# DeltaNet masks and output sums as PSUM accumulation, inverse copies on ScalarE

## The chip, the core and the metric

## The reference, cut to what matters

The model is a two-layer backbone over 512 latent and 256 context tokens, width 1024: a gated DeltaNet layer, then an attention layer, each followed by a mixer that picks experts by product keys. The change touches the DeltaNet layer's recurrence, which runs for 16 value heads of width 128, forwards and backwards in time, over chunks of tokens:

```python
gc = cumsum(gc)
decay = exp(where(incl, gc[:, None] - gc[None, :], -inf))     # incl: lower triangle
kk = k @ k.T
a = eye + where(strict, kk * decay * b[:, None], 0)
u, w = triangular_solve(a, [v * b, k * (b * exp(gc))])
v_new = u - w @ S
qk = where(incl, (q @ k.T) * decay, 0)
o = (q * exp(gc)) @ S + qk @ v_new
S = S * exp(g_last) + (k * exp(g_last - gc)).T @ v_new
```

The outputs of the forward and the backward direction are added. The state S left by the context is where the latents start.

## The kernel before

Everything is fp32; the large products outside the recurrence are split into two fp32r parts. The program is traced in one order and a scheduler places each engine's instructions by a model of their times, so an instruction can stand earlier or later on its engine than the text has it. Each engine then works through its own list in order. Tiles come from pools with a fixed number of buffers, and a write to a reused buffer waits for its last reader.

Chunks here are 128 tokens: 2 for the context, 4 for the latents. `dn_rec` (line 423) is called once for the context ("c") and once for the latents ("l"). It takes the 8 query/key heads in groups, 4 heads a group for the context and 2 for the latents, so that a group always holds 16 matrices per direction to invert. There are two groups for the context and four for the latents. The tiles of odd and even groups come from different pools, so that a group can be prepared while the group before it is still in its steps. The work on a group has four parts:

- Preparation, chunk by chunk (lines 450 to 472). `kk` in PSUM receives k·k and k·q (L453). VectorE multiplies both by the two triangle masks `tri` into `km` (L456), one mask per direction. `rp` in PSUM receives, for two value heads and two directions, the row of cumulated gates by a transpose of a broadcast column (L462). ScalarE forms `ar` = exp(-relu(gc - rp)) (L466, L467). VectorE multiplies into `U`, the matrix to invert (L470, four instructions), and `Ps` (named `Pm` in the rows), the masked and decayed k·q (L472).
- `dn_inv` (line 575): the inverse of I + U for 16 matrices and two directions at once. ScalarE gathers the 32x32 diagonal blocks (L585), VectorE transposes and eliminates them in 31 dependent steps (L596, L598) and transposes back (L602, L603). TensorE then builds the off-diagonal blocks with ScalarE copies between (`Tc`, `T6`), and VectorE copies the inverted diagonal blocks back into `U` (L639).
- `dn_step` (line 517), for each chunk, head and direction: `ks` = k·S and q·S (L529), `R` (L532), `yr` by the inverse (L540, L541), `vd` and `vn` (L545, L547), the state update `su` and `S` (L550, L555). Then `q`, the scaled q·S (L561, into `o` itself for the direction that comes first to a chunk, else into `qs`), `ops` = Ps·vn (L564), and VectorE's sums: q + ops (L571), and o + q for the direction that comes second (L573). In the context the first step of each direction has no state, and its `ops` are copied to `o` by ScalarE (L567).
- The end of a group: `o` is normalised (L503, L507), transposed (L513), multiplied by the gate `zt` loaded from memory (L510, L514), and stored (L515). `ZT` (8, 4) gives the buffers of `zt` for the context and the latents.

Beside the recurrence runs a background queue of gathers for the experts of the context. `tick` (line 55) is called at fixed places of the loops and issues gather steps by a rate. A step is an indirect DMA of 128 rows of 4 KB on GpSimd's queue (L965), into one of `GB` = 4 row buffers, and a VectorE instruction that reduces the row block against the tokens (L967).

The PSUM of `dn_rec` is one buffer each of `kk`, `rp` and `mg`, two of `ks`, and one each of `yr`, `su` (which shares with the transposes `tp`) and `ops`.

## Time and profile before

| | us |
|---|---|
| median of three runs | 4879.01 |
| the runs | 4902.33, 4879.01, 4874.26 |
| span of the profiled execution | 4891.1 |

The profiled execution was timed by its span alone: from the first to the last instruction that the profiler recorded. [...] Groups of instructions give the count, the busy time and the mean of one. A matmul of fp32 operands stands in the trace as two records.

| Stretch, us | What runs |
|---|---|
| 409 to 560 | last heads' projections, context groups prepared, first inverse |
| 560 to 700 | context steps, second inverse, ends of the groups |
| 700 to 919 | output product and routing of the context, latents' gate z |
| 919 to 1454 | latent recurrence, four groups, beside gathers |
| 1454 on | output product, routing, experts, attention layer, experts |

### The profile page before, as it was taken

The numbers are of one execution on the slowest core, as the hardware profiler recorded it, in microseconds if no ns is written. First come the engines' busy times: TensorE is split into PE (matmuls) and PEld (weight loads), VectorE is DVE, ScalarE is ACT, GpSimd is POOL, SyncE is SP. The second block draws the span as 40 slices with busy tenths as digits, with TensorE's granted clock in tenths as the row PEclk, the third lists the DMA queues.
The fourth block names the chain that finished last, engine by engine and source line by source line (L and its number), as shares of the span: only waits on it lengthen the run. The fifth ranks groups of instructions, "written<-read, shape, count | busy, mean of one in ns | idle before, by whom it ended". The sixth has DMA issues, their size and how long they took to land. (4 is left out here: it accounts for less than half of the span.)

```text
span 4891.1 us, 68996 instructions
## 1 busy us (share of the span) xinstructions
PE 4329.9 (89%) x24564; PEld 3455.1 (71%) x24564; DVE 3587.0 (73%) x8483; ACT 1866.5 (38%) x3605; POOL 1321.5 (27%) x1111
## 2 busy tenths in 40 slices
PE   6999669757569698999999999988997999999998
PEld 3778547545444556666788888745687998888887
DVE  4667825899965857566688888645579888888886
ACT  2335553447450213344333333223333554333333
POOL 0000000134344433222333334440000102444441
PEclk8999789768679899999999999999999999999999
DMA  7744246447578877777999999872133678999996
GB/s 296 261 150 135 75 144 191 153 148 254 177 242 317 301 240 268 269 260 272 329 349 351 339 339 337 292 268 74 61 112 107 215 260 287 355 334 335 336 324 230
DMA packets 480616, 1196.55 MB, mean 245 GB/s; under 512 B 40752, under 2 KB 239152, under 8 KB 470416
## 3 DMA queue, kind: packets, MB, share of 16 engines
q1 hardware_dynamic: 332816, 655.21, 38.2%
q0 software_dynamic: 147456, 536.94, 31.5%
q8 instruction: 194, 3.18, 0.3%
q14 instruction: 150, 1.23, 0.1%
HBM read 1079.50 MB, written 112.49 MB: 244 GB/s over the span
## 5 line engine op out<-in xcount | busy, mean ns | idle before, releaser
L965 POOL DMA_INDIRECT row<-in_peer_u,idx x512 | 613.2, 1198 | 1513.3 <-DVE row L967 706.3
L100 PE MATMUL up<-hil,uh 128*128 128x384 f32 x2048 | 709.4, 346 | 44.7 <-ACT c L1094 44.1
L102 PE MATMUL up<-hil,ul 128*128 128x384 f32 x2048 | 697.2, 340 | 0.0
L101 PE MATMUL up<-lol,uh 128*128 128x384 f32 x2048 | 696.1, 340 | 0.0
L100 PE MATMUL y<-vh,ch 128*128 128x512 f32 x1536 | 602.8, 393 | 9.1 <-ACT ch L106 7.6
L101 PE MATMUL y<-vl,ch 128*128 128x512 f32 x1536 | 602.9, 393 | 0.0
L102 PE MATMUL y<-vh,cl 128*128 128x512 f32 x1536 | 508.8, 391 | 0.0
L981 POOL DMA_INDIRECT row<-in_peer_v,idx x256 | 339.9, 1328 | 456.3 <-DVE lhs L984 374.5
L100 PEld LDWEIGHTS up<-hil,uh 128*128 128x128 f32 x2048 | 386.9, 189 | 94.8 <-ACT c L1094 65.4
L106 ACT CAST uh<-ur 128x1024 fp32r<-128x1024 f32 x256 | 268.3, 1048 | 454.3 <-PE up L101 322.3
L1017 POOL DMA_INDIRECT row<-in_peer_v,iT x256 | 279.5, 1092 | 557.7 <-PE yp L1020 473.7
L107 DVE TENSOR_TENSOR vl<-vr,vh 128x1024 fp32r<-128x1024 f32 x256 | 312.9, 1224 | 127.1 <-ACT vh L106 125.1
L106 ACT CAST vh<-vr 128x1024 fp32r<-128x1024 f32 x256 | 268.6, 1051 | 359.9 <-PE y L102 325.0
L101 PEld LDWEIGHTS up<-lol,uh 128*128 128x128 f32 x2048 | 387.1, 189 | 19.2 <-issue 10.9
L102 PEld LDWEIGHTS up<-hil,ul 128*128 128x128 f32 x2048 | 386.5, 189 | 18.2 <-issue 15.1
L107 DVE TENSOR_TENSOR ul<-ur,uh 128x1024 fp32r<-128x1024 f32 x256 | 312.1, 1220 | 74.7 <-ACT uh L106 70.1
L967 DVE SCALAR_TENSOR_TENSOR row<-row,ghs 128x1024 f32<-128x1024 f32 x256 | 311.2, 1222 | 73.7 <-DMA row<-in_peer_u,idx 72.7
L1066 DVE TENSOR_SCALAR A<-iotar,kt 128x128 f32<-128x128 f32 x768 | 221.8, 289 | 174.4 <-PE gp L1068 171.9
L100 PEld LDWEIGHTS y<-vh,ch 128*128 128x128 f32 x1536 | 289.8, 189 | 70.3 <-ACT ch L106 9.1
L102 PEld LDWEIGHTS y<-vh,cl 128*128 128x128 f32 x1536 | 288.6, 188 | 64.6 <-issue 4.2
L984 DVE SCALAR_TENSOR_TENSOR lhs<-row,lcf,lhs 128x1024 f32<-128x1024 f32 x254 | 325.1, 1280 | 9.6 <-DMA row<-in_peer_v,idx 8.0
L101 PEld LDWEIGHTS y<-vl,ch 128*128 128x128 f32 x1536 | 290.1, 189 | 56.3 <-issue 2.5
(397 smaller groups left out, 8788.1 us busy)
## 6 DMA issues: line engine op xcount, KB each, us to landing
ur<-in_uT SPq DMA_DIRECT2D x256, 512.0 KB
vr<-in_peer_v SPq DMA_DIRECT2D x256, 512.0 KB
w<-in_ada_w SPq DMA_DIRECT2D x48, 1024.0 KB
G_d<-st SPq DMA_DIRECT2D x10, 4096.0 KB
gt<-G_d SPq DMA_DIRECT2D x64, 640.0 KB
act_d<-c SPq DMA_DIRECT2D x129, 192.0 KB
c<-act_d SPq DMA_DIRECT2D x129, 192.0 KB
wr<-in_dn_w_in SPq DMA_DIRECT2D x48, 512.0 KB
```

The costliest lines, as they stand in the source:

```text
L100: first = mm(ps, lh, rh, start=start, stop=False)
L101: mm(ps, lh, rl, start=False, stop=False)
L102: mm(ps, ll, rh, start=False, stop=stop)
L106: self.nc.scalar.copy(hi, src)
L107: self.nc.vector.tensor_sub(lo, src, hi)
L965: nc.gpsimd.indirect_dma_start(out=u, out_offset=None, in_=self.I["peer_u"], in_offset=bass.IndirectOffsetOnAxis(ap=ix[:, k:k + 1], axis=0))
L967: mv = nc.vector.scalar_tensor_tensor(u, u, 1.0, hs, op0=ALU.mult, op1=ALU.mult, accum_out=coef[:, k:k + 1])
L981: nc.gpsimd.indirect_dma_start(out=v, out_offset=None, in_=self.I["peer_v"], in_offset=bass.IndirectOffsetOnAxis(ap=ix[:, k:k + 1], axis=0))
L984: keep(nc.vector.scalar_tensor_tensor(y, v, coef[:, k:k + 1], y, op0=ALU.mult, op1=ALU.add))
L1017: nc.gpsimd.indirect_dma_start(out=v, out_offset=None, in_=self.I["peer_v"], in_offset=bass.IndirectOffsetOnAxis(ap=iT[:, t:t + 1], axis=0))
L1066: nc.vector.tensor_scalar(A, iota, kt[:, 0, t:t + 1], None, op0=ALU.is_equal)
```

## The change

- The mask moves into `rp`. A constant `far` holds 0 inside the triangle and -1e30 outside. Each of the four quarters of `rp` is now two accumulated matmuls in place of a transpose: the broadcast gate column by the identity, then the identity by `far`. ScalarE's relu and exp then give 0 outside the triangle, and `km` with its VectorE product is gone.
- `U` and `Ps` read the unmasked products from `kk` in PSUM. `kk` is now one buffer for two chunks: both chunks' matmuls are issued at every even chunk.
- In `dn_step` `q` always goes to `qs`. The sums move into `ops`: identity times `o[:, c]` (when the other direction was there first) and identity times `q` are accumulated before Ps·vn, and one ScalarE copy brings `ops` to `o`.
- In `dn_inv` the copies of the diagonal blocks into `U` move from VectorE to ScalarE, and `Tc` and `T6` share one buffer.
- `ZT` goes from (8, 4) to (8, 2).
- Row buffers of the gathers are handed out by a new helper that can add pools of further buffers in three stages; the numbers of further buffers, `GM`, are 0, 0, 0.

The diff without the removed comments and without the renaming of the row buffers:

```diff
+        self.far = c.tile([P, 2, P], F32, name="far")
+        nc.vector.tensor_scalar(self.far, self.tri, 1e30, -1e30, op0=ALU.mult, op1=ALU.add)
...
+    def row(self):
+        p, n = self.slots[self.turn % len(self.slots)]
+        self.turn += 1
+        return p.tile([P, D], F32, name="row", tag="row", bufs=n)
...
-                        kk = pqp.tile([P, 2, P], F32, name="kk")
-                        nc.tensor.matmul(kk.rearrange("p a b -> p (a b)"), pk[:, c, 0, :],
-                                         pk[:, c, 0:2, :].rearrange("p a b -> p (a b)"), start=True, stop=True)
-                        km = pq.tile([P, 2, 2, P], F32, name="km", bufs=2)     # (kk, kq), dir
-                        nc.vector.tensor_mul(km, kk.unsqueeze(2).to_broadcast([P, 2, 2, P]), self.tri.unsqueeze(1).to_broadcast([P, 2, 2, P]))
+                        if c % 2 == 0:
+                            kk2 = pqp.tile([P, 2, 2, P], F32, name="kk")
+                            for cc in range(2):
+                                nc.tensor.matmul(kk2[:, cc].rearrange("p a b -> p (a b)"), pk[:, c + cc, 0, :],
+                                                 pk[:, c + cc, 0:2, :].rearrange("p a b -> p (a b)"), start=True, stop=True)
+                        kk = kk2[:, c % 2]
...
-                                nc.tensor.transpose(rp[:, v, d], gcol.to_broadcast([P, P]), self.ident)
+                                nc.tensor.matmul(rp[:, v, d], gcol.to_broadcast([P, P]), self.ident, start=True, stop=False)
+                                nc.tensor.matmul(rp[:, v, d], self.ident, self.far[:, d], start=False, stop=True)
...
-                                nc.vector.scalar_tensor_tensor(U[:, 2 * c + v, d], km[:, 0, d], G["b"][:, d, c0 + c, 2 * h + v:2 * h + v + 1],
+                                nc.vector.scalar_tensor_tensor(U[:, 2 * c + v, d], kk[:, 0], G["b"][:, d, c0 + c, 2 * h + v:2 * h + v + 1],
...
-                        nc.vector.tensor_mul(Ps[:, 2 * c:2 * c + 2], ar, km[:, 1:2].to_broadcast([P, 2, 2, P]))
+                        nc.vector.tensor_mul(Ps[:, 2 * c:2 * c + 2].rearrange("p v d t -> p (v d) t"), ar.rearrange("p v d t -> p (v d) t"), kk[:, 1:2].to_broadcast([P, 4, P]))
...
-            q = o[:, c] if fst else p.tile([P, 2, P], F32, name="qs", bufs=2)
+            q = p.tile([P, 2, P], F32, name="qs", bufs=2)
...
         ops = pqp.tile([P, 2, P], F32, name="ops")
+        rest = ([] if fst else [o[:, c]]) + ([] if z0 else [q])
         for v in range(2):
-            nc.tensor.matmul(ops[:, v], Ps[:, m0 + v, d], vn[:, v], start=True, stop=True)
-        if z0:
-            if fst:
-                nc.scalar.copy(o[:, c], ops)
-            else:
-                nc.vector.tensor_add(o[:, c], o[:, c], ops)
-            return
-        nc.vector.tensor_add(q, q, ops)
-        if not fst:
-            nc.vector.tensor_add(o[:, c], o[:, c], q)
+            for i, r in enumerate(rest):
+                nc.tensor.matmul(ops[:, v], self.ident, r[:, v], start=i == 0, stop=False)
+            nc.tensor.matmul(ops[:, v], Ps[:, m0 + v, d], vn[:, v], start=not rest, stop=True)
+        nc.scalar.copy(o[:, c], ops)
...
-        Tc = p.tile([P, M, 32], F32, name="Tc")
+        Tc = p.tile([P, M, 32], F32, name="Tc", tag="T6", bufs=1)
...
-                    nc.vector.tensor_copy(U[sl(b), :, d, sl(b)], Yc[d][sl(b), ms])
+                    nc.scalar.copy(U[sl(b), :, d, sl(b)], Yc[d][sl(b), ms])
...
-        T6 = p.tile([P, M, 64], F32, name="T6")
+        T6 = p.tile([P, M, 64], F32, name="T6", tag="T6", bufs=1)
...
-ZT = 8, 4
+ZT = 8, 2
+GM = 0, 0, 0
```

## Rows read from the trace of the kernel before

**Rows 1.** The page, part 1: span, then busy time, share and instructions by engine.

```profile
span 4891.1 us, 68996 instructions
...
PE 4329.9 (89%) x24564; PEld 3455.1 (71%) x24564; DVE 3587.0 (73%) x8483; ACT 1866.5 (38%) x3605; POOL 1321.5 (27%) x1111
```

**Rows 2.** View by windows: stretch, length, busy (instructions) by engine, PEclk, DMA share, GB/s.

```profile
409.00:500.00 91.00, 86.26 (x594) 78.85 (x594) 74.27 (x136) 56.63 (x132) 6.35 (x6) 0.98 0.54 162
500.00:560.00 60.00, 29.82 (x535) 22.62 (x533) 44.69 (x126) 30.04 (x88) 1.10 (x2) 0.63 0.29 104
560.00:700.00 140.00, 104.38 (x1056) 83.75 (x1056) 71.00 (x203) 96.00 (x350) 8.21 (x8) 0.84 0.14 47
...
919.00:1000.00 81.00, 38.88 (x124) 25.06 (x124) 70.94 (x160) 41.38 (x118) 16.64 (x16) 0.56 0.49 177
1000.00:1045.00 45.00, 13.93 (x482) 12.24 (x483) 39.33 (x82) 16.00 (x35) 21.62 (x17) 0.50 0.48 157
1045.00:1120.00 75.00, 60.81 (x719) 50.09 (x720) 70.43 (x183) 48.96 (x171) 25.14 (x23) 0.84 0.58 190
1120.00:1200.00 80.00, 62.02 (x432) 52.38 (x427) 76.19 (x175) 57.98 (x197) 40.34 (x39) 0.87 0.82 270
1200.00:1260.00 60.00, 22.50 (x78) 14.60 (x77) 51.57 (x129) 25.53 (x95) 18.83 (x15) 0.63 0.58 198
1260.00:1360.00 100.00, 67.50 (x1168) 57.86 (x1168) 92.71 (x218) 58.03 (x186) 40.18 (x37) 0.72 0.55 174
1360.00:1454.00 94.00, 63.05 (x432) 50.33 (x432) 64.42 (x134) 60.18 (x215) 48.43 (x41) 0.83 0.72 247
919.00:1454.00 535.00, 328.70 (x3424) 262.56 (x3424) 465.58 (x1075) 308.07 (x1014) 211.19 (x185) 0.73 0.61 205
```

**Rows 3.** View of waits, 860 to 1460 us: total us, times, longest.

```profile
POOL row L965 <- DVE row L967: 220.2, 98, 29.7
...
DVE row L967 <- DMA row<-in_peer_u,idx: 30.9, 36, 3.1
```

**Rows 4.** VectorE groups by form, 860 to 1460 us: busy us, mean ns.

```profile
L456 DVE TENSOR_TENSOR km<-kk,tri 128x512 f32<-128x512 f32 x32 | 21.9, 685 | 10.0 <-PE kk L453 10.0
L472 DVE TENSOR_TENSOR Pm<-ar,km 128x512 f32<-128x512 f32 x32 | 21.9, 684 | 0.0
L639 DVE COPY U<-R 32x256 f32<-32x256 f32 x64 | 18.6, 291 | 0.9
...
L573 DVE TENSOR_TENSOR o<-o,qs 128x256 f32<-128x256 f32 x32 | 13.4, 418 | 0.2
L571 DVE TENSOR_TENSOR qs<-qs,ops 128x256 f32<-128x256 f32 x32 | 13.2, 414 | 3.3 <-PE ops L564 3.3
L571 DVE TENSOR_TENSOR o<-o,ops 128x256 f32<-128x256 f32 x32 | 13.2, 414 | 0.2 <-PE ops L564 0.2
```

**Rows 5.** Groups of work, 860 to 1460 us, ScalarE, same columns.

```profile
L585 ACT COPY Uc<-U 32x256 f32<-32x256 f32 x64 | 25.7, 402 | 4.1 <-DVE U L470 3.4
```

**Rows 6.** Tile ops, whole run: ns min/median/max, first and last start, forms.

```profile
L564 PE MATMUL ops<-vn,Pm x384: 272/275/582, 567.5 to 1438.0; 128*128 128x128 f32 x192
...
L567 ACT COPY o<-ops x16: 372/372/431, 568.5 to 659.8; 128x256 f32<-128x256 f32 x16
```

**Rows 7.** Timeline of TensorE, 1139 to 1149 us (start, us, what, records).

```profile
1139.75 0.60 PE L462 MATMUL rp<-ident,Ggc 128*128 128x128 f32 x4
...
1148.28 0.39 PE L541 MATMUL yr<-R,U 128*128 128x128 f32 x2
...
1148.50 0.39 PE L540 MATMUL yr<-pk,U 128*128 128x128 f32 x2
```

**Rows 8.** Timeline of VectorE, 946 to 965 us, first and last of six.

```profile
946.85 0.69 DVE L456 TENSOR_TENSOR km<-kk,tri 128x512 f32<-128x512 f32 x1 [1.78 <-PE kk L453]
...
964.62 0.69 DVE L456 TENSOR_TENSOR km<-kk,tri 128x512 f32<-128x512 f32 x1
```

**Rows 9.** Timeline of the SP queue at the end of the latent recurrence.

```profile
1445.62 7.58 SPq L515 DMA_DIRECT2D og_l<-zt  x4
```

## The prediction

> **What bounds the kernel now.** I read the page's busy shares first. TensorE is busy 89% of the span and VectorE 73% [rows 1], but these are means over stages with different limits, and the chain that ended last runs only through the final expert stage, so it says nothing of the DeltaNet part. I therefore cut the stretch in which the changed lines run into windows [rows 2]. The latent recurrence lasts from 919 to 1454 us. In its 535 us VectorE is busy 465.6 us (87%), TensorE 328.7 (61%, at a mean granted clock of 0.73) and ScalarE 308.1 (58%). From 919 to 1360 us VectorE is at 86 to 95% in every window. Only the last stretch, 1360 to 1454, has no leader: 64, 63 and 60 us of 94.

> The waits agree: the gathers' queue on GpSimd waits 220.2 us for the VectorE instruction that empties a row, while VectorE waits for a gathered row only 30.9 us [rows 3]. So in this stage VectorE sets the pace. The context part is different: between 409 and 500 us TensorE is at 95%, between 560 and 700 no engine is above 75% (104.4 of 140 us), which is a chain of short dependent steps.

> **What the change takes from VectorE.** Durations are means of rows 4. In the latent stage: 32 mask products km at 0.685 us, 21.9 us; 64 copies of the inverse's diagonal blocks (L639) at 0.291 us, 18.6 us; the output sums, 64 of L571 at 0.414 and 32 of L573 at 0.418 us, 39.8 us. Together 80.3 us of 465.6. In the context: 16 masks, 11.0 us; 16 steps with both sums, 13.3 us; and 64 smaller copies, at most 18.6 us by the same row.

> The remaining products now read kk from PSUM instead of km from SBUF. Rows 4 hold the same shape both ways: L456 reads PSUM and takes 685 ns, L472 reads SBUF and takes 684; L571 (PSUM) takes 414, L573 (SBUF) 418. I cost the move at nothing. [...]

> **What it adds to TensorE.** A matmul here is two records: ops has 384 for 192 matmuls [rows 6]; the transposes it replaces are one each. Two consecutive two-record yr matmuls start 0.22 us apart in a fast stretch [rows 7], so one record costs 0.11 us at clock 1.0, and 0.11 divided by the clock below that. Each chunk's rp goes from 4 records to 16: 12 x 0.11 = 1.3 us, 32 chunks, 42 us. Each step adds 4 records (its q), and 4 more where o is already there: per group of 16 steps 8 x 4 + 8 x 8 = 96 records, 10.6 us, four groups, 42 us. Latent sum 84 us at full clock, 116 at the mean clock of 0.73. Context: 16 x 12 records, 21 us, and 16 steps with 8 each, 14 us.

> **What it adds to ScalarE.** The copy o<-ops has a price in the trace, 0.372 us [rows 6]: 64 latent ones, 23.8 us. The inverse's copies have the shape of Uc<-U, 0.402 us [rows 5]: 64, 25.7 us. ScalarE goes from 308 to 358 us. In the inverse the next reader of these copies is the last multiplication, so they can run while TensorE works; cover gone, 16 x 0.402 = 6.4 us per inverse.

> **Buffers and waits.** kk is now held until the second chunk's Pm product, and the next pair's matmuls wait for that. Behind them on TensorE stand the rp matmuls, and VectorE's U products wait for both. Today such a wait for kk cost 1.78 us where it shows [rows 8], and 10.0 us in all [rows 4]. With gather rows to reduce in between I take it as covered; uncovered, 16 pairs x 1.78 = 28 us. The rp buffer is single: its matmuls took 0.60 us for 4 records [rows 7] and will take 0.60 + 1.3 = 1.9 us. The chunk pace is (964.62 - 946.85) / 5 = 3.55 us [rows 8], so at full clock this fits, and at half clock (3.8 us before ScalarE even starts to read) it does not. Two zt buffers in place of four make the second head's loads wait on SP for the first head's stores, with the next group's loads queued behind; the last four stores are spread over 7.58 us [rows 9], so the bounds are 0 and 7.6; it counts once, at the end, and I take 2. Tc and T6 sharing a buffer, and the one constant at the start, cost nothing: Tc's last reader always precedes T6, and the constant is made while the first weights load.

> **The sum by stretch.** A stretch's new length is its old one times (largest new busy time / largest old busy time), that is, the leading engine keeps its share. It is worked twice, with TensorE at full clock and at the clock of rows 2; I choose between them.
> - 919 to 1000 (16 chunks): VectorE 70.9 to 59.9, TensorE 38.9 to 76.6 at clock 0.56 (21.1 / 0.56 more), 43 at 1.0. Change -12.6 to +6.5; taken -3, the clock rising with the denser work.
> - 1000 to 1045 (inverse): VectorE 39.3 to 34.7, ScalarE 16 to 22.4. -5.3 to +6.4; taken -2.
> - 1045 to 1120 (steps, inverse): VectorE 70.4 to 55.8, TensorE 60.8 x 0.84 + 10.6 = 61.7 or 73.4. -9.3 to +3.2; taken -3.
> - 1120 to 1200 (8 chunks, steps): VectorE 76.2 to 60.7, TensorE 62.0 x 0.87 + 21.2 = 75 or 86.4. -1.3 to +10.7; taken +4.
> - 1200 to 1260 (8 chunks): VectorE 51.6 to 46.1. -6.4 to 0; taken -4.
> - 1260 to 1360 (two inverses, steps): VectorE 92.7 to 73.4; ScalarE 58.0 + 6.0 + 12.8 = 76.8 now leads. -17.2 to 0; taken -10.
> - 1360 to 1454 (last steps, tail): VectorE's 10 us go, TensorE 63 to 75.8 at its clock, ScalarE 60 to 66. 0 to +16.6; taken +3, the zt wait in it.

> Latent sum -15, bounds -52 and +43. Context: 409 to 500, 8 chunks x 1.3 = +10.6 on an engine at 95%, bounds 0 and 10.6, taken +5; 500 to 560, bounds -5 and +5, taken 0; 560 to 700, TensorE +14 at full clock, 17 at 0.84, against 13.3 us off VectorE, bounds -5 and +17, taken +1. Context +6, bounds -10 and +33. Net -9: the profiled execution's span of 4891.1 would be 4882. That span lies 12.1 us above the median of 4879.01 and inside the three runs (4874.26 to 4902.33); I apply the difference to the median: 4870. Later stages keep their instructions and their gather steps, so the difference is carried to the end unchanged.

> **Rivals.**
> 1. *TensorE becomes the bound at a low clock* (the slower one). Place: the chunk loop and the step loop. All upper ends: latent +43, context +33, 4879 + 76 = 4955. For it: granted clock 0.50 to 0.63 in three of the seven windows [rows 2], 84 us of new work in an in-order queue, ops now also waiting for q. Against: the windows with the densest TensorE work already run at 0.84 and above. It decides once TensorE stays under about 0.7 while its busy share passes 90%. Chance 0.18 for more than +1%.
> 2. *VectorE simply gets shorter*, the clock rises, and everything else fits beneath. All lower ends: -52, context 0: 4827. If even VectorE's share of 87% were kept with no new leader, 535 x 80.3 / 465.6 = -92: 4787. For it: the 87 to 95% shares and the 220.2 us of gather waits. Against: in the step stretches the three engines are already nearly level. Chance 0.22.
> 3. *Nothing is taken from the path*, what VectorE loses TensorE and ScalarE gain step by step: -15 to +40, around 4879. This is my forecast with its neighbours, chance 0.60.
> 4. *The kk pair stalls*: +28 us latent, 14 in the context on top of the forecast, 4912; inside 3's neighbourhood, 0.06 of its 0.60.

> **How the numbers follow.** The three runs spread 0.6%, so 1% (49 us) is about what a measurement can tell from no change. Faster by over 1% is rival 2 (0.22), slower rival 1 (0.18), within 1% the rest (0.60). The likeliest case alone is 4845 to 4915. For eight in ten the range reaches part way into both rivals: 4805 to 4930.

> **What would show it.** Right: from 919 on, VectorE's busy sum falls by about 80 us while TensorE's rises by 85 to 115 and ScalarE's by 50; the latent stage lasts 500 to 545 us with no engine above 80%; rp has 768 records. Rival 1 shows as a clock near 0.5 in the chunk stretches and ScalarE's first product waiting for rp; rival 2 as a stage under 490 us and a clock above 0.85; rival 4 as VectorE idle before U, released by kk. Wrong in kind would be a difference outside 409 to 1454 us, for instance another order of gathers in the later stages.

## The result and the profile after

| | before | after |
|---|---|---|
| median of four runs, us | 4877.29 (4874.26 to 4902.33) | 4949.91 (4944.66 to 4963.01) |
| ratio, 95% interval | | 1.0138 (1.0118 to 1.0159) |
| last store of the context's outputs, us into the profile | 694.1 | 712.5 |
| first cast of expert indices (start of the latent stage) | 918.7 | 940.0 |
| last store of the latents' outputs (its end) | 1452.9 | 1516.8 |
| latent stage | 534.2 | 576.8 |
| from there to the last output | 3433.0 | 3439.2 |

The change made the kernel 1.4% slower: 4950 us against a forecast of 4870 and a range up to 4930. The loss is in two places, 21 us ahead of the latent stage and 43 us in it. What follows it is 6 us longer; over all profiles of this study that part varies between 3404 and 3439 us although no edit touches it, so nothing is read from it. In the experiments, therefore, the medians tell the total, and the stage (start and end read as in the table, from one profile each) tells the place. Inside the stage the starts of the four inverses (VectorE's transposes into `UB`) show where the 43 us arise: up to the first 1 us, then 4, 15 and -1 us, and 23 us behind the start of the last.

The page's busy times (answering to [rows 1]) and the window of the latent stage (to the last row of [rows 2]; PE, PEld, DVE, ACT, POOL, clock, DMA share, GB/s), after:

```profile
span 4961.2 us, 71036 instructions
...
PE 4422.0 (89%) x25652; PEld 3574.6 (72%) x25652; DVE 3489.7 (70%) x8180; ACT 1936.6 (39%) x3813; POOL 1333.1 (27%) x1111
```

```profile
940.00:1518.00 578.00, 392.86 (x4192) 347.61 (x4192) 402.80 (x885) 353.25 (x1142) 208.21 (x185) 0.82 0.59 190
```

VectorE fell from 465.6 to 402.8 us, TensorE rose from 328.7 to 392.9 with the granted clock up from 0.73 to 0.82 (TensorE's, as a share of full speed, mean of the stage), ScalarE from 308.1 to 353.3. No engine is above 70% of the stage, against 87% before, and the stage is 8% longer. Now its waits, after (total us, times, longest; [rows 3]):

```profile
POOL row L980 <- DVE row L982: 259.5, 89, 27.6
...
DVE row L982 <- DMA row<-in_peer_u,idx: 73.1, 49, 10.5
DVE S L575 <- PE su L570: 46.5, 19, 8.0
...
ACT qs L581 <- PE ops L586: 30.9, 36, 3.9
```

The time that VectorE was given back it spends waiting: 73.1 us for gathered rows (30.9 before) and 46.5 us for the state update's matmul (2.8 before). ScalarE has a new wait of 30.9 us, for the matmul that adds `q` into `ops`: with two `qs` buffers the next `q` can't be written before. GpSimd's wait for VectorE *grew*, from 220.2 to 259.5, although VectorE has less to do.

The wait for `su` is not due to the mask's matmuls: u_mask, the changed kernel with the masks back on VectorE (experiments below), still has 43.1 us of it. It takes the sums and the copies together: without the inverse's copies on ScalarE 10.1 us are left (u_copies), without the sums 9.1 (u_sums). The line of u_mask:

```profile
DVE S L573 <- PE su L568: 43.1, 14, 8.1
```

One of the longer waits shows how. The timeline after, behind the elimination of an inverse, beside the steps of another group (start, length, what, records, in brackets idle time):

```profile
1105.94 0.39 PE L561 MATMUL yr<-R,U 128*128 128x128 f32 x2
...
1107.01 1.23 ACT L654 COPY U<-R 32x256 f32<-32x256 f32 x3
...
1112.51 0.62 ACT L565 ACTIVATE vd<-yr,Gbkd 128x128 f32<-128x128 f32 x2
...
1113.18 0.70 PE L570 MATMUL su<-vd,pk 128*128 128x256 f32 x2 [2.23 <-ACT vd L565]
...
1113.92 0.61 DVE L575 SCALAR_TENSOR_TENSOR S<-S,Gegl,su 128x128 f32<-128x128 f32 x2 [4.87 <-PE su L570]
```

The step's `yr` is done at 1106.3, but ScalarE comes to `vd` only at 1112.5. Between them in its list stand eight of the inverse's copies (3.3 us) and other copies; TensorE's `su` waits for `vd`, and VectorE for `su`.

### The profile page after: what moved, and what is told of

The parts are those of the page before. It is cut to its first block, busy times and chain, and to the rows that moved or that the text cites. A ratio compares the mean times of both kernels' runs of the same rounds, so it can differ in the third digit from the quotient of the medians.

```text
span 4961.2 us, 71036 instructions
## 1 busy us (share of the span) xinstructions
PE 4422.0 (89%) x25652; PEld 3574.6 (72%) x25652; DVE 3489.7 (70%) x8180; ACT 1936.6 (39%) x3813; POOL 1333.1 (27%) x1111
## 5 line engine op out<-in xcount | busy, mean ns | idle before, releaser
L996 POOL DMA_INDIRECT row<-in_peer_v,idx x256 | 352.6, 1377 | 439.9 <-DVE lhs L999 372.2
```

Source lines behind the costliest of these rows:

```text
L996: nc.gpsimd.indirect_dma_start(out=v, out_offset=None, in_=self.I["peer_v"], in_offset=bass.IndirectOffsetOnAxis(ap=ix[:, k:k + 1], axis=0))
```

## The experiments

Each was compared with runs of the kernel before on the same chip (medians 4883 to 4890; 4877 for the changed kernel). "Stage" is the length of the latent stage, before 534.2 and after 576.8. The expectations, printed as they were on record, name their theories themselves. Every edit also lets the scheduler place all instructions anew, so each difference holds the edit and the new order together.

### One part undone, one part done

Three kernels undo one part of the changed kernel, three do one part alone on the kernel before. Their edits are the hunks of the diff shown ahead, taken back or applied:

```diff
 # u_sums (after) / reversed in o_sums (before): dn_step
-        nc.scalar.copy(o[:, c], ops)                # and the identity matmuls
+        nc.vector.tensor_add(q, q, ops)             # and o + q
 # u_copies / reversed in o_copies: dn_inv
-                    nc.scalar.copy(U[sl(b), :, d, sl(b)], Yc[d][sl(b), ms])
+                    nc.vector.tensor_copy(U[sl(b), :, d, sl(b)], Yc[d][sl(b), ms])
 # u_mask / reversed in o_mask: rp by one transpose, kk per chunk, km
-                                nc.tensor.matmul(rp[:, v, d], self.ident, self.far[:, d], start=False, stop=True)
+                                nc.tensor.transpose(rp[:, v, d], gcol.to_broadcast([P, P]), self.ident)
```

> The changed kernel with the output sums back on VectorE (q into o for the first direction, two adds), everything else as changed. Theory S, the sums on TensorE lengthen the step stretches: in the changed trace the first latent step stretch lasts 86 us in place of 55, ScalarE waits 30.9 us for the qs buffer and VectorE's state update 46.5 us for su. Then this run comes back by 40 to 60 us, to 4890 to 4910. Theory C, the inverse's copies on ScalarE delay the chain of the inverse: this run stays within 15 us of 4950. Theory M, the mask matmuls: likewise within 15 us of 4950.

> The changed kernel with the copies of the inverted diagonal blocks back on VectorE. Theory C: 16 or 32 copies of 0.3 to 0.4 us stand on ScalarE ahead of the copy Tc, for which TensorE waits (Tc starts 9 us after its matmuls end in the changed trace, 5 before); six inverses give back 30 to 60 us, 4890 to 4920. Theory S: 5 to 15 us, 4935 to 4945. Theory M: under 15 us.

> The changed kernel with the masks back on VectorE (km, transposes into rp, kk for one chunk). Theory M, the twelve further records a chunk and the longer hold of rp and kk set the pace: 30 to 60 us come back, 4890 to 4920. Theories S and C: VectorE has 33 us more to do again and little is gained, 4935 to 4975.

> The kernel before with only the output sums moved to TensorE accumulation and ScalarE. Theory S: slower than before by 35 to 60 us, 4912 to 4937. Theories C and M: within 15 us of 4877, or faster by up to 30 since VectorE loses 40 us in the latent stage.

> The kernel before with only the inverse's diagonal copies on ScalarE. Undoing them gained 37 us, undoing the sums 38, undoing the masks 13, in sum 88 of a loss of 66 to 72; doing the sums alone cost 13. If each part has its own price in any company, this run is slower than before by 25 to 40 us. If the parts aggravate each other, because ScalarE and TensorE have slack as long as only one of them is loaded, it is slower by 5 to 20.

> The kernel before with only the masks in PSUM and the shared kk buffer. If each part has its own price: slower by 5 to 15 us. If the parts aggravate each other: the same as before within 10 us or faster by up to 20, since VectorE loses 33 us and ScalarE gets nothing to do.

| kernel | ratio to before | start of stage | stage | against |
|---|---|---|---|---|
| u_sums | 1.0064 (1.0041 to 1.0087) | 935.7 | 554.3 | after: -22.5 |
| u_copies | 1.0070 (1.0051 to 1.0090) | 933.3 | 553.9 | after: -22.9 |
| u_mask | 1.0121 (1.0100 to 1.0143) | 925.2 | 573.3 | after: -3.5 |
| o_sums | 1.0026 (1.0010 to 1.0041) | 921.9 | 554.6 | before: +20.4 |
| o_copies | 1.0034 (1.0018 to 1.0049) | 925.6 | 548.6 | before: +14.4 |
| o_mask | 0.9999 (0.9984 to 1.0015) | 928.2 | 528.9 | before: -5.3 |

In the latent stage the sums alone cost 20 us, the copies 14, and the mask gains 5: 29.5 together, against 42.6 for all three. Sums and copies without the mask (u_mask) cost 39.1, 4 more than their parts, and beside them the mask gains nothing any more. Ahead of the stage the starts shift by 3, 7 and 9.5 us, together 20 of the 21.3, so the mask loses there more than the 5 us that it gains later. No part alone makes the kernel faster.

Of the expectations, u_copies (4913 us) met theory C and u_mask (4936) met S and C, so M was wrong. Theory S was not met: u_sums came to 4912, just above its 4910, and o_sums cost 13 us where it asked for 35 and more. The three alone add 0.6% by their medians and the whole change 1.4%, so the parts aggravate each other, as the second theories of o_copies and o_mask had it. The smaller sharing (two `zt` buffers, one for `Tc` and `T6`) was not run alone; gm_before and gm_mask below have it, with further row buffers, and their stages are within 1 us of those without.

The window of o_sums shows the pattern of the whole change:

```profile
922.00:1478.00 556.00, 376.60 (x3811) 315.73 (x3809) 438.39 (x981) 330.51 (x1079) 216.68 (x185) 0.75 0.60 198
```

VectorE has 27 us less to do than before, and the stage is 20 us longer.

### Buffers and order

If ScalarE's wait for `qs` were the cause, more buffers would cure it; if the inverse's copies cost because they stand ahead of `Tc` on ScalarE, moving them behind would.

```diff
 # q4 (after) and o_sums_q4 (o_sums)
-            q = p.tile([P, 2, P], F32, name="qs", bufs=2)
+            q = p.tile([P, 2, P], F32, name="qs", bufs=4)
 # c_late (after): the copies in a loop of their own, behind the products that fill U
+                    self.tc.keep_in_program_order(nc.scalar.copy(U[sl(b), :, d, sl(b)], Yc[d][sl(b), ms]))
 # o_mask_lat (before): o_mask for the latents only, the context as before
```

> The changed kernel with four buffers for qs in place of two. The trace of the changed kernel has ScalarE waiting 30.9 us, 36 times, for TensorE to finish with a qs buffer, with the next steps' R, vd and vn queued behind. If that wait is what the sums cost, 20 to 35 us come back, 4915 to 4930. If it is the further records on TensorE, or the order of the steps, under 8 us, 4942 to 4952.

> The kernel before with only the output sums moved, and four qs buffers in place of two. The sums alone cost 0.26% with 29.1 us of ScalarE waits for a qs buffer in the latent stage. If the buffer wait is the larger part of their price: at or below before, 0.998 to 1.001. If it is the smaller part: 1.001 to 1.0025.

> The changed kernel with the copies of the diagonal blocks still on ScalarE, but held behind Tc, the two products into Z64 and the products into U, by program order. If the copies cost by standing ahead of Tc (Tc starts 7 to 9 us after its matmuls end, against 0 to 5 before): 15 to 35 us come back, 4915 to 4935. If they cost wherever they stand on ScalarE, because T6 then waits for them: under 10 us, 4940 to 4955.

> The kernel before with the masks in PSUM and the shared kk buffer for the latents alone; the context keeps km. With the masks everywhere the latent stage was 5 us shorter and the context 9.5 us longer. If these add: the latent stage 5 us shorter and the context as before, so 0.997 to 0.9995; if the shorter latent stage was chance, 1.000.

q4: 1.0103 (1.0079 to 1.0127), stage 570.3. o_sums_q4: 1.0045 (1.0030 to 1.0060), stage 551.6, no better in total than o_sums and above both of its forecasts. The wait for `qs` is mostly a symptom: in o_sums ScalarE waits 29.1 us for `qs`, in o_sums_q4 23.0 us for `ops` itself, one instruction later. c_late: 1.0093 (1.0069 to 1.0118), stage 573.3: by its profile the order of the copies is worth about 3 us of the 23 that u_copies gives back, although VectorE's wait for `su` falls from 46.5 to 26.7 us, for the wait for rows grows from 73.1 to 85.0. By the ratios c_late and q4 stand 0.45 and 0.35% below the changed kernel's 1.0138, some 20 us, but those were compared on another chip, and up to the end of the latent stage their profiles are only 7 us shorter. So the size of both stays loose. o_mask_lat: 1.0003 (0.9988 to 1.0019), stage 532.4: without the context's loss the mask is still level, so its gain in the latent stage is at the limit of what can be told.

### What a microsecond of each engine costs

These add work of one engine to the kernel before, at the place of the sums, that changes no result; x_sums takes the sums away with nothing in their place.

```diff
 # o_pe: as many identity matmuls into ops as the change adds, from a tile of zeros; sums stay on VectorE
+                nc.tensor.matmul(ops[:, v], self.ident, self.zer, start=i == 0, stop=False)
 # o_act
+            nc.scalar.copy(p.tile([P, 2, P], F32, name="scr", bufs=2), ops)
 # o_dve
+            nc.vector.tensor_copy(p.tile([P, 2, P], F32, name="scr", bufs=2), ops)
 # x_sums
-        nc.vector.tensor_add(q, q, ops)
-        if not fst:
-            nc.vector.tensor_add(o[:, c], o[:, c], q)
```

> The kernel before, sums on VectorE as they were, but as many identity matmuls as the changed kernel has are accumulated into ops from a tile of zeros, which waits for nothing. It prices the records on TensorE alone: 512 of them, 56 us at full clock. If TensorE's queue is what lengthens the step stretches (theory P): the latent stage grows by 15 to 30 us and the time by 0.3 to 0.6%. If it is the new order of waits, q and o before the product, qs held until TensorE has read it, and the copy to o by ScalarE (theory W): under 8 us, since the clock rises with the added records.

> The kernel before, sums on VectorE as they were, with one further ScalarE copy of ops to a scratch tile in each step with a state, 80 of 0.37 us or 30 us. It prices ScalarE's load alone. If ScalarE's queue carries the recurrence, so that each instruction more on it lengthens a step: the latent stage grows by 12 to 24 us, 0.2 to 0.5%. If ScalarE has slack there: under 6 us.

> The kernel before with one further VectorE copy of ops to a scratch tile in each step that has a state (64 in the latent stage, 16 in the context); nothing reads the scratch tile. It is the counterpart of o_act (the same copy on ScalarE: latent stage +14 us) and o_pe (identity matmuls: +21 us). At about 0.41 us (the nearest row, L571, has the same operand sizes) it adds 26 us to VectorE in the latent stage. Theory A (the step chain goes through three nearly level engines, VectorE is not the one that sets the pace): the stage grows by 0 to 10 us, less than for ScalarE. Theory B (VectorE does set the pace, and the change only lost its gain to work added elsewhere): the stage grows by 22 to 28 us, a us per us. Between them, 10 to 22, a us on either engine costs about the same.

> The kernel before with the output sums L571 and L573 left out, so the recurrence's output lacks the term Ps.vn and, for the second direction, q; no engine gets work in their place. In the latent stage VectorE loses 40 us of its 466 (39.8 by rows 4), in the context 13.3. This is the change's gain alone, without its price. Theory A: the latent stage shortens by 0 to 15 us, so that moving the sums had little to win from the start. Theory B: it shortens by 35 to 46 us (a us per us, up to the share rule), and the gain was lost to the identity matmuls and the ScalarE copy (together +35 when added alone to the kernel before).

| kernel | ratio to before | stage | change of the stage | work added or taken | change of that engine's busy time |
|---|---|---|---|---|---|
| o_pe | 1.0045 (1.0031 to 1.0060) | 555.1 | +20.9 | 384 records, 42 / 0.77 = 55 us at its clock | TensorE +34.5 |
| o_act | 1.0040 (1.0026 to 1.0055) | 548.0 | +13.8 | 64 copies, 25.3 us | ScalarE +18.9 |
| o_dve | 1.0045 (1.0032 to 1.0058) | 557.9 | +23.7 | 64 copies, 26.6 us | VectorE +21.8 |
| x_sums | 0.9977 (0.9962 to 0.9993) | 528.3 | -5.9 | 96 sums, 39.8 us | VectorE -27.2 |

(TensorE's busy time rose by less than its work since the clock rose from 0.73 to 0.77.) The windows of o_dve, then of x_sums:

```profile
919.00:1478.00 559.00, 336.75 (x3424) 269.23 (x3424) 487.37 (x1141) 308.80 (x1014) 206.82 (x185) 0.70 0.61 196
```

```profile
915.00:1445.00 530.00, 320.01 (x3429) 259.82 (x3427) 438.43 (x982) 303.86 (x1015) 219.82 (x185) 0.76 0.63 207
```

This is the main finding. VectorE time added costs a microsecond for a microsecond (23.7 us for 21.8), as theory B wants. VectorE time taken away, with nothing put elsewhere, gives back a fifth (5.9 of 27.2), as theory A wants. By these two runs VectorE did lead before, but by a few microseconds only. And the two engines that were to take the work at 61% and 58% busy were not free: of what each got, two fifths (20.9 of 55) and a half (13.8 of 25.3) show in the stage. Nothing uses the added results, but some work has to wait for them. The matmuls of o_pe go into `ops` ahead of Ps·vn, and VectorE's sums wait 16.3 us for `ops` (3.5 before); in o_act the sums stand behind the extra copy and wait 6.0 us for it. ScalarE's extra copy shows how, in its group of o_act (count, busy, mean ns, idle time before it):

```profile
L566 ACT COPY scr<-ops 128x256 f32<-128x256 f32 x64 | 25.3, 395 | 15.0 <-PE ops L564 14.8
```

`ops` is the last result of a step: the copies hold ScalarE for 14.8 us until `ops` comes, and what ScalarE has next in its list, the `R`, `vd` and `vn` of other steps among it, stands behind, as `vd` stood from 1106.3 to 1112.5 us behind the inverse's and other copies in the changed kernel.

A rival to these prices was not separated: the order. Compared with before, 14% of VectorE's and 30% of ScalarE's remaining instructions in the stage of x_sums stand outside the longest sequence that both kernels share (by operation and tile). That need not cost anything: with 12 and 13% moved, gm_before below is within 1 us of before. But no run took the sums away with the order held, so part of the missing gain may be the new order.

### What limits the stage just below VectorE

In x_sums VectorE waits 54.1 us for gathered rows, in the changed kernel 73.1. If the gathers take over when VectorE gets lighter, further row buffers should bring the gain out. The changed kernel has a parameter for them; the kernel before got the helper and the shared buffers that make the room.

```diff
-GM = 0, 0, 0
+GM = 3, 0, 0        # gm_after, and gm_mask (after without sums and copies); 2, 0, 0 in gm_before and gm_xsums
```

> The changed kernel with three further row buffers for the gathers during the latent recurrence (GM = 3, 0, 0; seven in place of four). In the changed kernel VectorE waits 73.1 us there for a gathered row to land, against 30.9 before. Theory G (gathers cap the stage once VectorE is lighter: a row can be requested only when a buffer is free, so a lighter VectorE only waits for rows): that wait falls under 25 us and the latent stage of 577 us shortens by 20 to 45. Theory A (step chain through TensorE and ScalarE sets it): the wait falls, but the stage changes by less than 8 us, other waits growing in its place.

> The kernel before with the sums L571 and L573 left out (the recurrence's output lacks Ps.vn), two zt buffers instead of four, a shared Tc/T6, and two further row buffers in the latent recurrence (six in place of four). Without the further buffers the 40 us taken from VectorE shortened the stage by 6 (528 against 534), and the wait for rows grew from 30.9 to 54.1 us. Theory G: the stage falls to 490 to 510 us, the gain showing once rows land in time. Theory A: 522 to 532.

> The kernel before with two further row buffers in the latent recurrence (with two zt buffers and a shared Tc/T6 to make room). It prices the buffers alone. Theory G, with VectorE as the limit of before: 0 to -8 us, since its row wait is 30.9 us in all and VectorE is at 87%. Theory A: also near 0. A larger gain, 15 us and more, would say that the gathers limit the kernel before as well.

> The part of the change that cost nothing in the latent stage (masks in PSUM, paired kk: 528.9 us against 534.2, VectorE 18 us lighter), without the sums and the copies, with three further row buffers. The candidate for a version faster than both. Theory G: latent stage 500 to 515, the whole kernel 0.3 to 0.6% faster than before. Theory A: stage 522 to 532, the whole kernel level with before (ratio 0.998 to 1.002), as o_mask alone was.

| kernel | ratio to before | stage | without the further buffers | wait for rows |
|---|---|---|---|---|
| gm_after | 1.0100 (1.0064 to 1.0135) | 562.0 | 576.8 | 38.1 (73.1) |
| gm_xsums | 0.9987 (0.9965 to 1.0009) | 518.4 | 528.3 | 25.7 (54.1) |
| gm_before | 1.0003 (0.9983 to 1.0023) | 533.3 | 534.2 | 23.3 (30.9) |
| gm_mask | 1.0028 (1.0008 to 1.0048) | 528.1 | 528.9 (o_mask) | 21.1 |

The waits of gm_xsums:

```profile
DVE row L982 <- DMA row<-in_peer_u,idx: 25.7, 16, 6.0
...
DVE S L573 <- PE su L568: 20.3, 16, 2.9
```

For gm_after and gm_xsums both theories missed: the stage falls by 15 and 10 us, more than the 8 of the one and less than the 20 of the other. The buffers halve the wait for rows, but the stage gets only 10 to 15 of the 28 to 35 us; in gm_xsums VectorE's wait for `su` rose from 10.8 to 20.3 us instead. So there seem to be two limits close below VectorE: the gathers with four row buffers, and the step chain through TensorE and ScalarE. With sums gone and rows in time the stage is 16 us shorter for 27 us of VectorE work. In the kernel before the buffers bring nothing, as both theories had it. No version beat both kernels by a measurable amount: gm_mask, the candidate, has the stage that theory A forecast and is level with before or slightly slower, and gm_xsums leaves work out.

## Why the prediction was wrong, point by point

**Durations and counts held.** The groups that answer to [rows 4 to 6], after:

```profile
L490 DVE SCALAR_TENSOR_TENSOR U<-kk,Gb,ar 128x128 f32<-128x128 f32 x128 | 36.6, 346 | 16.9 <-PE kk L473 11.4 <-ACT ar L487 2.8 <-ACT ar L486 2.7
...
L492 DVE TENSOR_TENSOR Pm<-ar,kk 128x512 f32<-128x512 f32 x32 | 21.8, 680 | 0.0
...
L534 DVE SCALAR_TENSOR_TENSOR zt<-tp,ngc,zt 128x512 f32<-128x512 f32 x16 | 12.0, 749 | 17.4 <-PE tp L533 11.1 <-DMA zt<-zt_d 6.3
```

```profile
L654 ACT COPY U<-R 32x256 f32<-32x256 f32 x64 | 25.7, 402 | 0.8
L588 ACT COPY o<-ops 128x256 f32<-128x256 f32 x64 | 24.2, 379 | 5.2 <-PE ops L587 2.7 <-PE tp L533 2.5
```

```profile
L481 PE MATMUL rp<-ident,Ggc 128*128 128x128 f32 x256 | 57.5, 310 | 38.5 <-ACT ar L486 37.0 <-DVE z L437 1.4
L482 PE MATMUL rp<-far,ident 128*128 128x128 f32 x256 | 55.0, 300 | 0.0
...
L586 PE MATMUL ops<-qs,ident 128*128 128x128 f32 x256 | 52.6, 289 | 0.1
...
L586 PE MATMUL ops<-o,ident 128*128 128x128 f32 x128 | 26.9, 293 | 0.1
```

The products that read `kk` in PSUM take 346 and 680 ns where those that read `km` in SBUF took 345 and 684, so the move was free, as costed. The copies take 402 and 379 ns, foreseen 402 and 372: ScalarE gained 45 us, foreseen 50. The 384 further `rp` records and 384 of `ops` in this stage are those counted. TensorE's new work is 84 us at full clock; before's 328.7 us scaled to the new clock are 328.7 x 0.73 / 0.82 = 293, and 293 + 84 / 0.82 = 395, measured 392.9. So the sign "TensorE's rises by 85 to 115" failed (64 us): the higher clock shortened the old work, while the count was right. The wait for `kk` stayed at 11.4 us (10.0 before): rival 4 did not come. The `zt` wait cost VectorE 6.3 us, taken as 2 within 0 to 7.6.

**VectorE's saving was mis-sized.** Step: "Together 80.3 us of 465.6". Busy time fell by 62.8. The means of a group are not what an instruction costs its engine. VectorE's timeline before, in an inverse with other work between:

```profile
1056.86 0.60 DVE L555 SCALAR_TENSOR_TENSOR S<-S,Gegl,su 128x128 f32<-128x128 f32 x2
1057.38 0.42 DVE L596 TENSOR_TENSOR itmp<-Yb,UB 128x256 f32<-128x256 f32 x1
1057.71 0.41 DVE L571 TENSOR_TENSOR o<-o,ops 128x256 f32<-128x256 f32 x1
1058.05 1.22 DVE L967 SCALAR_TENSOR_TENSOR row<-row,ghs 128x1024 f32<-128x1024 f32 x1
```

The sum at 1057.71 lasts 0.41 us, but the next instruction starts 0.34 us after it: it overlaps the end. Added over all forms the groups' times of the stage are 517 us where the busy time is 465.6. So 80.3 us of such times were divided by 465.6 us of a union that holds 517 us of them. Each part alone took less busy time than its durations: the sums 27.2 of 39.8 us (x_sums), the masks 18 of 21.9 (o_mask), the copies 15 of 18.6 (o_copies).

**The rule of the sum failed.** Step: "the leading engine keeps its share", with -10 taken for 1260 to 1360 and -15 for the whole stage. (In 1260 to 1360 it was also misapplied: at that stretch's clock TensorE's 67.5 + 10.6 / 0.72 = 82 us would lead, not ScalarE's 76.8.) It makes a stretch shorter in proportion to VectorE's work until another engine's *busy time* takes the lead. x_sums tests it with no price on the other side: -27 us of busy time, at a share of 87%, should give -31; it gave -6 (with the scheduler's new order in it). Busy shares of 61 and 58% hid that TensorE and ScalarE are on the same chain, `ks`, `R`, `yr`, `vd`, `su`, `S`, and that a step's end feeds the next. The prediction priced their new work only by whether it made them the leader; o_pe, o_act and o_copies (14.4 of 25.7 us, net of what VectorE lost) show that about 40 to 55% of it was paid long before that. The terms that this mis-sized are those of the steps (+4, -10 and +3 for 1120 to 1200 and from 1260 on; the sums alone measured +20) and of the inverse's copies, put under "they can run while TensorE works" with 6.4 us per inverse if not (25.6 in four): measured alone +14.4.

The mask was rightly taken as near nothing in this stage (-3 and -4 in the two stretches of chunks alone; -5 measured alone), though it has half of the TensorE records. Its matmuls run in the chunk loops, where TensorE has time: it waits there 37.0 us for ScalarE to free `rp`.

**The reading of the waits.** Step: "the gathers' queue on GpSimd waits 220.2 us for the VectorE instruction that empties a row ... So in this stage VectorE sets the pace". In the changed kernel the same wait is 259.5 us, with 63 us less VectorE work; in o_dve, with 22 us more, it is 257.5. It says that the reduce hasn't run, not why: it stands in VectorE's list behind instructions that wait for others. o_dve (24 us for 22) agrees that VectorE set the pace; x_sums (6 us for 27) shows how little relief can follow.

**The context** was forecast at +6 within -10 to +33 and came to +21. The mechanism named for 409 to 500 us, 10.6 us on a TensorE at 95%, reached further than costed. SP's timeline, before and then after (start, time over which the issues spread, what):

```profile
500.39 8.14 SPq L275 DMA_DIRECT2D zt_d<-zt  x4
510.14 3.64 SPq L510 DMA_DIRECT2D zt<-zt_d  x8
513.82 1.93 SPq L446 DMA_DIRECT2D pk<-pk_d  x4
```

```profile
512.98 25.31 SPq L293 DMA_DIRECT2D zt_d<-zt  x5
539.97 4.49 SPq L530 DMA_DIRECT2D zt<-zt_d  x8
544.50 2.16 SPq L464 DMA_DIRECT2D pk<-pk_d  x4
```

The context's gates `z` are finished later, their stores hold SP, and the second group's `pk` loads behind them are issued at 544.5 in place of 513.8, 31 us late. The mask alone does the same: `pk` at 539.9 in o_mask, whose context ends 13 us late. The rest of the 18 us at the context's end comes from the sums and copies: in u_mask `pk` is on time (515.7), and the context still ends 9 us late. The prediction looked at SP for the `zt` of the latents, not here.

**The rivals.** Rival 1 named nearly the time, 4955, but not the cause: its point of decision was a TensorE under 0.7 of the clock and over 90% busy, and it is at 0.82 and 68%. Rival 2 has lost most of its ground: with half of the 80 us taken away and nothing added (x_sums) the stage shortens by 6 us, with row buffers by 16, where keeping VectorE's share would give 31; all 80 us were not tried. The forecast's own case, "what VectorE loses TensorE and ScalarE gain step by step", is the right mechanism with the wrong balance: -15 to +40 was allowed as its span, and +64 came. The upper ends of the latent stage add up to +43, almost exactly what came, and that is luck: they stand for TensorE or ScalarE leading by busy time, but over the stage VectorE still has the most (402.8 us); and 23 us of the growth lie behind the start of the last inverse, where they allowed 17.

What stays open: how much of each price is the new order of instructions; why the mask, 5 us to the good alone, is 3.5 us to the bad beside sums and copies, and how the copies of the inverse cost what they do, since moving them behind `Tc` (c_late) takes 20 us off the wait for `su` but by its profile only 3 off the stage. The gathers' limit was shown by the buffers, the step chain as the other one only by the waits that grow.

## What to carry to other kernels

An engine at 87% of a stage may lead by only a few microseconds: before moving work off it, leave that work out once and see what the stage gives back, and add it once to the receiver and see what it takes. In this recurrence, whose steps pass through three engines, work given to an engine at 60% was still paid for by two fifths to a half; levelling the busy shares was no gain by itself. Where a scheduler reorders, compare the orders too, or hold them, before a difference is put down to the work. A wait of a gather queue for the engine that frees its buffers doesn't say that this engine is overloaded; see whether the wait shrinks when its work does.

## What the runs showed of the hardware

Consecutive VectorE instructions that do not read each other's results overlapped in the trace of before by 0.07 and 0.09 us (0.41 long, 0.34 apart, and 0.42 long, 0.33 apart, at 1057.4 to 1058.1 us), and the times of the groups add up to 517 us within 465.6 us of busy time; a sum removed gave back about 0.3 us of busy time (27.2 us for 96) where its row says 0.41 to 0.42. Two accumulated fp32 matmuls in place of a transpose of 128 columns cost four records in place of one: 0.44 us, as pairs of records start 0.22 us apart in the changed kernel (1189.5 to 1190.9 us, at a granted clock of 1.00). In before, four records of `rp` took 0.44 us to the start of the next matmul at a granted clock of 1.00 (948.37 to 948.81 us) and 0.91 us at 0.50 (956.65 to 957.56 us): 0.11 and 0.23 us a record. The granted clock, as the mean of the latent stage, was 0.73 before and higher in these four with work added to TensorE (0.75 in o_sums, 0.77 in o_pe, 0.82 in o_mask and after), and the stage still got longer in three of them; in x_sums it was 0.76 with no matmul added, in a shorter stage.
